# Four moves in the order of work of a two-layer decoder trunk: the first weight block, the second triangular inverse, the last products of v, and the last norm

## The chip, the cores and the metric

The kernel runs on one core of one Trainium2 chip, as one program that is launched once. A core has a matrix engine (TensorE, "PE" in the profile, with its weight loads shown apart as "PEld"), a vector engine (DVE), a scalar engine (ACT), a general engine (POOL), a queue engine (SP) that here only issues DMAs, and 16 DMA engines. Each engine runs its own list of instructions strictly in order; an instruction that waits holds back all that stand behind it on the same engine. The metric is the device time of one execution in microseconds (us), median over executions; lower is better.

## The reference

The input is 512 tokens of 1024 numbers. Layer 0 is an RG-LRU block and layer 1 an RWKV-7 block; each is followed by a gated convolution MLP, and a last RMS norm ends it. Cut to what matters here:

```python
h = rmsnorm(x);  u = h @ w_in + b_in                    # RG-LRU: the first products of the kernel
...                                                     # conv, gates, scan, w_out, residual, MLP 0
r, k, v = (h + xx * mix[i]) @ w_rkv[i]  for i in 0,1,2  # RWKV-7
for t in tokens:                                        # state S of 64 x 64 for each of 16 heads
    S = S * w[t] + (S @ a[t]) b[t]^T + v[t] k[t]^T
    y[t] = S @ r[t]
y = groupnorm(y) * ln_w + ln_b + bonus * v              # the norm: 64 numbers of a head and token
x = x + (y * g) @ w_out                                 # then MLP 1 and the last norm
```

The recurrence is computed in chunks of 64 tokens. In a chunk the tokens depend on each other through a triangular matrix of 64 x 64 for each head, whose inverse is needed before the chunk can be done.

## The kernel before, in words

**Products.** Every large product is taken in three passes (`mm3`, lines 46 to 53): the weight and the activation are each split in a high part (a cast on ACT, line 90) and a low part (a subtraction on DVE, line 91), and PE adds high x high (L51), high x low (L52) and low x high (L53). Weights come by DMA in blocks of 512 KB ("raw", L148), are split into "wh" and "wl", and are used by `project_gen` (L172), which walks over blocks of 256 rows (`c`), four output banks (`o`) and the two halves of a block (`k`). `next_weights` (L165) asks for the loads of the next three blocks and the split of the next two each time a block is taken.

**The order of the work.** The program is written as generators that are interleaved by hand: `push(task, lane)` puts one into one of three lists, and `background(n, lane)` takes n pieces from the first task in that list. In the chunk steps the amounts are in `self.fills`: three lanes, and for each the pieces taken at three places in a step. What is written in this way is the priority only. A planner then lays out the list of each engine: it plays the program through with its own costs, gives a free engine the earliest written of the instructions that it takes to be ready, and hands out the buffers (`b4`, 21 of 4 KB a partition; PSUM, eight banks). So a list can differ from the written order where the planner believed that a transfer or another engine would be done earlier or later. `keep_in_program_order` ties an instruction behind the one written before it on its engine.

**Start.** `load_x` (L308) issues the loads of x (`xin`, four pieces, the first in two halves) and of the first weights in turn. The input is transposed on PE into "xT" (L344), block by block of 128 of the 1024 features, and then split on ACT (L346) and DVE (L347) into "xs". `warm` (L332) puts transposes of the identity on PE that nothing uses. `lru` (L359) does block 0, splits weight block 0 in two halves, calls `warm(WARM2)`, does block 1, and pushes blocks 2 to 7 as a task for the first products.

**Inverse.** `solve(H)` (L997) makes the inverses for one half of the heads: eight groups of small products ("aab", L1020) with copies on ACT (L1025, L1028), a transpose on DVE (L1033), a chain of 31 pairs of DVE operations (L1041, L1043), two more DVE transposes (L1046, L1048), and two rounds of small products ("m1p" L1065, "ltp" L1077). The tiles of the first inverse are named D and A, those of the second DA.

**Products of v.** `tokens(g)` (through `project_tokens`, L977) computes v for all tokens and a quarter of the features: 96 products (L989 to L991), given out in 16 pieces of six. Groups 0 and 1 are done before the chunk steps, groups 2 and 3 are pushed to lane 1 as cover for the steps.

**Chunk steps.** There are 16 chunks of work (8 for each half H of the heads; `NC` is 8) and two groups of heads, the second one chunk behind the first, so 17 steps (`step`, L1190). The chain in a step is: "pe" on PE (L1206), a copy on ACT (L1209), "pu" on PE (L1222), a copy on ACT (L1229, tile "tu"), "pd" on PE (L1238), two operations on DVE (L1247, L1248 or L1250, tile "sv"), and the next "pe". Between them PE does "s", "tr" and "py". After every second step a `tail` (L1262) is begun: the group norm of 128 tokens, in three parts: mean, square and variance, with a power on POOL (L1278); three DVE operations (L1281 to L1283); transposes on PE ("pz", L1288) with ACT copies (L1291). `trail` moves each open tail one part on, in the next steps.

**End of the block.** `first_half` (L1362), pushed in lane 1 after step 9, multiplies the first half of y by the gate ("pgt" on PE, "yg" on DVE at L1356, split into "BK") and runs its 96 output products, in 20 pieces; the second half follows after the last step, from line 1421 to line 1441.

## Time and profile before

| what | value |
|---|---|
| median of 3 runs | 1327.06 us (1325.48 to 1329.35) |
| the profiled execution, its own time | 1328.46 us |
| its span, first to last instruction | 1326.7 us |
| so around the span | 1.76 us |
| mean granted PE clock | 0.992 |
| PE busy | 1295.2 us, 98% |
| DVE busy | 860.3 us, 65% |
| ACT busy | 614.0 us, 46% |
| POOL busy | 67.9 us, 5% |
| DMA | 120.27 MB, mean 91 GB/s |

Times inside the profile count from the start of the span. In the rows with several columns each engine has its busy time and, in brackets, its number of instructions in the stretch; "PEclk" is the granted clock as a share of full speed. "[3.35 <-DMA xin]" behind an instruction says that its engine had stood idle for 3.35 us and what ended that. PE is shown as busy at half clock too, so a lower clock has to be read in its own column.

### The profile page before, as it was taken

To read this page: it belongs to the slowest core of one execution; us is meant where nothing else is said; L and a number is where in the kernel's file an instruction comes from. 1 tells how busy PE (TensorE), PEld (TensorE's weight loads), DVE (VectorE), ACT (ScalarE), POOL (GpSimd) and SP (SyncE) were. 2 spreads that over 40 slices of the span, in tenths; PEclk is the share of its full clock that TensorE was granted. 3 is DMA by queue.
4 is the path that set the end of the run, shared out by engine and by line. 5 is a ranking of instruction groups with operands and counts; after the bars stand their busy time and mean duration, and the time that the engine had idled before them with its cause. 6 is when DMAs were issued, how large, how long until landed. Compare 5 with 4: busy or idle time off the path is not lost.

```text
span 1326.7 us, 20245 instructions
## 1 busy us (share of the span) xinstructions
PE 1295.2 (98%) x8339; PEld 1055.3 (80%) x8339; DVE 860.3 (65%) x1332; ACT 614.0 (46%) x968; POOL 67.9 (5%) x110
## 2 busy tenths in 40 slices
PE   8999999999999999999999988799999999999998
PEld 7877888888888888876678877678888888888886
DVE  5998656455436655497989787877565555365523
ACT  6797444333224423368843668555533332244311
POOL 4000000000000000020010011120000000000000
PEclk8999999999999999999999999899999999999999
DMA  5423333323333433213212112133323223333311
GB/s 183 126 64 96 96 111 96 95 64 96 95 96 95 127 115 120 88 32 116 86 48 72 58 38 80 42 89 91 99 89 109 67 95 95 96 96 127 112 64 64
DMA packets 72124, 120.27 MB, mean 91 GB/s; under 512 B 9498, under 2 KB 21476, under 8 KB 71904
## 3 DMA queue, kind: packets, MB, share of 16 engines
q1 hardware_dynamic: 70672, 117.20, 28.7%
q8 instruction: 65, 1.06, 0.3%
q10 hardware_dynamic: 576, 1.05, 0.2%
q0 software_dynamic: 784, 0.74, 0.2%
q14 instruction: 27, 0.22, 0.1%
HBM read 114.44 MB, written 4.52 MB: 90 GB/s over the span
## 4 chain that ended last, share of the span: by engine, by line
PE 88%; DVE 6%; ACT 3%; issue 1%; DMA 1%; POOL 0%; SPq 0%; POOLq 0%; DVEq 0%; ACTq 0%
PE acc L51 22%; PE acc L53 22%; PE acc L52 22%; PE acc L616 3%; PE acc L615 3%; PE acc L617 3%; PE s L1160 1%; PE acc L989 1%; PE acc L990 1%; PE acc L991 1%; PE pe L1206 1%; DVE W L1167 1%; DMA xin<-in_x_dram 1%; DVE X L1043 1%; DVE sv L1248 1%
## 5 line engine op out<-in xcount | busy, mean ns | idle before, releaser
L51 PE MATMUL acc<-xs,wh 128*128 128x512 f32 x896 | 352.0, 393 | 0.0
L53 PE MATMUL acc<-xs,wl 128*128 128x512 f32 x896 | 348.9, 390 | 0.7 <-DVE wl L91 0.7
L52 PE MATMUL acc<-xs,wh 128*128 128x512 f32 x896 | 349.6, 390 | 0.0
L91 DVE TENSOR_TENSOR wl<-raw,wh 128x1024 fp32r<-128x1024 f32 (+1 forms) x201 | 242.9, 1216 | 163.4 <-PE acc L52 95.0
L90 ACT CAST wh<-raw 128x1024 fp32r<-128x1024 f32 (+1 forms) x201 | 207.9, 1045 | 257.7 <-DVE wl L91 169.6
L53 PEld LDWEIGHTS acc<-xs,wl 128*128 128x128 f32 x896 | 168.5, 188 | 36.8 <-DVE wl L91 1.2
L51 PEld LDWEIGHTS acc<-xs,wh 128*128 128x128 f32 x896 | 168.8, 188 | 35.0 <-ACT wh L90 0.2
L52 PEld LDWEIGHTS acc<-xs,wh 128*128 128x128 f32 x896 | 168.7, 188 | 34.5 <-DVE wl L91 0.2
L576 DVE SCALAR_TENSOR_TENSOR cv<-gpad,pv,cv 128x512 f32<-128x512 f32 x96 | 71.9, 749 | 22.2 <-ACT cv L574 21.1
L90 ACT CAST hid<-un 128x512 fp32r<-128x512 f32 x48 | 29.8, 620 | 108.7 <-DVE un L583 108.7
L616 PE MATMUL acc<-wh,hid 128*128 128x512 f32 (+1 forms) x200 | 76.8, 384 | 0.0
L615 PE MATMUL acc<-wh,hid 128*128 128x512 f32 (+1 forms) x200 | 76.5, 382 | 0.0
L617 PE MATMUL acc<-wl,hid 128*128 128x512 f32 (+1 forms) x200 | 75.9, 380 | 0.0
L52 PE MATMUL acc<-hid,wh 128*128 128x512 f32 x192 | 75.7, 394 | 0.0
L53 PE MATMUL acc<-hid,wl 128*128 128x512 f32 x192 | 75.6, 394 | 0.0
L51 PE MATMUL acc<-hid,wh 128*128 128x512 f32 x192 | 75.5, 393 | 0.0
L582 DVE TENSOR_TENSOR un<-acc,rb 128x512 f32<-128x512 f32 x48 | 33.1, 689 | 44.3 <-PE acc L53 44.3
L91 DVE TENSOR_TENSOR hid<-un,hid 128x512 fp32r<-128x512 f32 x48 | 33.2, 691 | 31.5 <-ACT hid L90 31.5
L574 ACT ACTIVATE cv<-gpad,pv 128x512 f32<-128x512 f32 x48 | 39.2, 817 | 20.3 <-DVE gpad L571 20.1
L578 ACT ACTIVATE ge<-cv 128x512 f32<-128x512 f32 x48 | 30.1, 627 | 35.6 <-DVE cv L576 35.6
L620 DVE TENSOR_TENSOR xtok<-xtok,acc 128x512 f32<-128x512 f32 (+1 forms) x25 | 16.7, 666 | 44.9 <-PE acc L617 44.9
L615 PEld LDWEIGHTS acc<-wh,hid 128*128 128x128 f32 x200 | 37.5, 188 | 8.0
(425 smaller groups left out, 2176.1 us busy)
## 6 DMA issues: line engine op xcount, KB each, us to landing
raw<-in_ffn_w_up_dram SPq DMA_DIRECT2D x96, 512.0 KB, 3.9
raw<-in_ffn_w_down_dram SPq DMA_DIRECT2D x48, 512.0 KB, 3.7
raw<-in_rwkv_w_rkv_dram SPq DMA_DIRECT2D x24, 512.0 KB, 3.8
raw<-in_lru_w_in_dram SPq DMA_DIRECT2D x16, 512.0 KB, 3.9
raw<-in_lru_w_out_dram SPq DMA_DIRECT2D x8, 512.0 KB, 3.8
raw<-in_rwkv_w_out_dram SPq DMA_DIRECT2D x8, 512.0 KB, 3.4
xd<-x SPq DMA_DIRECT2D x8, 256.0 KB, 2.0
AR<-xd SPq DMA_DIRECT2D x1, 2048.0 KB, 9.1
```

The source lines that it names most:

```text
L51: nc.tensor.matmul(ps, wh, xh, start=start, stop=False)
L52: nc.tensor.matmul(ps, wh, xl, start=False, stop=False)
L53: nc.tensor.matmul(ps, wl, xh, start=False, stop=stop)
L90: (self.nc.vector.tensor_copy if dve else self.nc.scalar.copy)(hi, src)
L91: self.nc.vector.tensor_tensor(lo, src, hi.bitcast(F32), ALU.subtract)
L574: nc.scalar.activation(cv, gp[:, 0:T], AF.Identity, bias=self.vec(f"ffn_conv_b{l}", fb), scale=cw(0))
L576: nc.vector.scalar_tensor_tensor(cv, gp[:, j : j + T], cw(j), cv, ALU.mult, ALU.add)
L578: nc.scalar.activation(ges[o], cv, AF.Gelu_apprx_tanh)
L582: nc.vector.tensor_tensor(un, ps, rbs[0], ALU.mult)
L615: nc.tensor.matmul(ps, hh[:, s], wh[:, k, m], start=kk == 0, stop=False)
L616: nc.tensor.matmul(ps, hl[:, s], wh[:, k, m], start=False, stop=False)
L617: nc.tensor.matmul(ps, hh[:, s], wl[:, k, m], start=False, stop=kk == 7)
```

## The change

- The pad `WARM2` goes from 4 to 20 transposes. Block 1 of x is no longer done ahead of the first products: with the new argument `early`, the first products of weight block 0 run for `k` = 0 over all four banks, and block 1 is written after the second of these banks. The call of `next_weights`, which also splits weight block 1, is thereby written ahead of block 1.
- The second inverse is pushed after the seventh piece of the first group of v, where it was pushed at the start of the second group: ten calls of `background` earlier, each with 0.8 pieces for lane 2.
- Step 7 no longer asks for all of v first, only that one task is left in lane 1; the last group of v may run on in step 7, and what is left of it is taken at the first place of step 8. The fills of steps 0 to 6 go from 3.8 to 3.4 pieces in lane 1 and from 5.1 to 4.5 in lane 2. In steps 10 and 11 lane 1 gets 2.8 pieces for 2.1 before; from step 12 on 2.1 as before.
- The last tail is split by groups of heads: one for the first two blocks after step 15, one for the other two after step 16, each with half the elements. Gate products of blocks 4 and 5 are multiplied ahead of the third part of the second of them.

```diff
-WARM2 = 4
+WARM2 = 20
...
-    def project_gen(self, xs, evac, nob=4, kb=8, kc=2, join=2):
+    def project_gen(self, xs, evac, nob=4, kb=8, kc=2, join=2, early=None):
...
             ws = [self.next_weights() for _ in cs]
+            if early and cs[0] == 0:
+                (wh, wl), = ws
+                for o in range(nob):
+                    self.mm3(pss[o], (wh[:, 0, o * P : (o + 1) * P], wl[:, 0, o * P : (o + 1) * P]), xs[0], True, False)
+                    if o == 1:
+                        early()
             for o in range(nob):
                 for c, (wh, wl) in zip(cs, ws):
-                    for k in range(kc):
+                    for k in range(1 if early and c == 0 else 0, kc):
...
             warm(WARM2)
-            block(1)
...
-                self.project(xs, lambda o, ps: take(g * 4 + o, ps), after=None if g else first, rate=1.2, join=2 if g else 1)
+                self.project(xs, lambda o, ps: take(g * 4 + o, ps), after=None if g else first, rate=1.2, join=2 if g else 1,
+                             early=None if g else lambda: block(1))
...
-        def tail(H, c2):
-            y = ytok[H, c2].rearrange("p b (h i) -> p (b h) i", h=2)
+        def tail(H, c2, b0=0, nb=4):
+            hs = slice(2 * b0, 2 * (b0 + nb))
+            y = ytok[H, c2][:, b0 : b0 + nb].rearrange("p b (h i) -> p (b h) i", h=2)
...
         for g in range(2):
-            if g:
-                self.push(self.solve(1, AR, BK, LTs), 2)
             for i, _ in enumerate(tokens(g)):
+                if g == 0 and i == 6:
+                    self.push(self.solve(1, AR, BK, LTs), 2)
...
-        self.fills = ((1.2, 1.1, 0.2), (1.0, 0.9, 1.9), (1.3, 1.8, 2.0))
+        self.fills = ((1.2, 1.1, 0.2), (0.9, 0.8, 1.7), (1.1, 1.6, 1.8))
...
         for n in range(N + 1):
-            while n == NC - 1 and self.tasks[1]:
+            while n == NC - 1 and len(self.tasks[1]) > 1:
                 self.background(1, 1)
             if n == NC:
-                self.drain()
-                self.fills = ((2.9, 0.5, 2.3), (0.8, 0, 1.3), (0, 0, 0))
+                for lane in (0, 2):
+                    while self.tasks[lane]:
+                        self.background(1, lane)
+                self.fills = ((0, 0, 0), (32, 0, 0), (0, 0, 0))
             if n == NC + 1:
                 load_lnw(1)
+                self.drain()
+            if n > NC:
+                self.fills = ((0, 0, 0), (1.2, 0, 1.6) if n < NC + 4 else (0.8, 0, 1.3), (0, 0, 0))
             step(n, trail)
             m = n - 1
-            if m > 0 and m % 2:
+            if n >= N - 1:
+                tails.append(tail(1, NC // 2 - 1, 2 * (n - N + 1), 2))
+                next(tails[-1])
+            elif m > 0 and m % 2:
                 tails.append(tail(m // NC, m % NC // 2))
                 next(tails[-1])
...
         trail()
         gp = [gate_mm(b) for b in range(4, 8)]
-        self.background(3, 1)
+        self.background(2.5, 1)
+        for i in range(2):
+            gate_mul(4 + i, gp[i])
         trail()
-        self.background(1, 1)
-        gate_mul(4, gp[0])
         self.drain()
-        for i in range(1, 4):
+        for i in range(2, 4):
             gate_mul(4 + i, gp[i])
```

More of the change, by code (lines that the diff above doesn't have):

```diff
@@ L1260, in step @@
             fill(2)
-        def tail(H, c2):
-            y = ytok[H, c2].rearrange("p b (h i) -> p (b h) i", h=2)
-            wide = lambda ap: ap.unsqueeze(2).to_broadcast([P, 8, C])
-            sm = lambda name: self.xsp.tile([P, 8, C], F32, tag="sq", name=name, bufs=3)
-            mu, var = (pool.tile([P, 8], F32, tag=k, name=k, bufs=2) for k in ("mu", "var"))
+        def tail(H, c2, b0=0, nb=4):
+            hs = slice(2 * b0, 2 * (b0 + nb))
+            y = ytok[H, c2][:, b0 : b0 + nb].rearrange("p b (h i) -> p (b h) i", h=2)
+            wide = lambda ap: ap.unsqueeze(2).to_broadcast([P, 2 * nb, C])
+            sm = lambda name: self.xsp.tile([P, 8, C], F32, tag="sq", name=name, bufs=3)[:, 0 : 2 * nb]
+            mu, var = (pool.tile([P, 8], F32, tag=k, name=k, bufs=2)[:, 0 : 2 * nb] for k in ("mu", "var"))
             self.need(("bonus", H))
@@ L1272, in tail @@
             nc.scalar.activation(sq, y, AF.Square)
-            vv = V[:, c2, H * 512 : H * 512 + 512].rearrange("p (b i) -> p b i", i=C)
+            vv = V[:, c2, H * 512 + b0 * P : H * 512 + (b0 + nb) * P].rearrange("p (b i) -> p b i", i=C)
             bv = sm("bv")
-            nc.gpsimd.tensor_tensor(bv, vv, wide(bons[H][:, c2, :]), ALU.mult)
+            nc.gpsimd.tensor_tensor(bv, vv, wide(bons[H][:, c2, hs]), ALU.mult)
             nc.vector.tensor_reduce(var, sq, AX.X, ALU.add)
             nc.vector.tensor_scalar(var, var, 1.0 / C, GN_EPS, ALU.mult, ALU.add)
-            nc.gpsimd.tensor_tensor(mu, var, self.mhalf.to_broadcast([P, 8]), ALU.pow)
+            nc.gpsimd.tensor_tensor(mu, var, self.mhalf.to_broadcast([P, 2 * nb]), ALU.pow)
             yield 1
             tc.keep_in_program_order(nc.vector.tensor_tensor(y, y, wide(mu), ALU.mult))
-            nc.vector.tensor_tensor(y, y, lnws[H], ALU.mult)
+            nc.vector.tensor_tensor(y, y, lnws[H][:, hs], ALU.mult)
             nc.vector.tensor_tensor(y, y, bv, ALU.add)
@@ L1285, in tail @@
             pz = self.bank("pz")
-            for i in range(4):
-                put = tc.keep_in_program_order if i == 0 else lambda ins: ins
+            for i in range(b0, b0 + nb):
+                put = tc.keep_in_program_order if i == b0 else lambda ins: ins
                 put(nc.tensor.transpose(pz[:, i * P : (i + 1) * P], ytok[H, c2][:, i, :], self.ident))
-            for i in range(4):
+            for i in range(b0, b0 + nb):
                 b = H * 4 + i
```

## The prediction, made before the changed kernel was run

> **What bounds the kernel now.** I read the page's busy shares first, then PE's own list of waits over the whole span.
>
> ```profile
> PE 1295.2 (98%) x8339; PEld 1055.3 (80%) x8339; DVE 860.3 (65%) x1332; ACT 614.0 (46%) x968; POOL 67.9 (5%) x110
> ```
> ```profile
> PE pe L1206 <- DVE sv L1248: 6.7, 7, 2.9
> PE pd L1238 <- ACT tu L1229: 4.9, 6, 1.5
> PE xT L344 <- DMA xin<-in_x_dram: 3.3, 1, 3.3
> PE pz L1288 <- DVE ytok L1283: 2.9, 1, 2.9
> ...
> PE m1p L1065 <- DVE XN L1048: 1.5, 1, 1.5
> ...
> PE acc L53 <- DVE wl L91: 0.7, 1, 0.7
> ```
>
> PE is the bound, and no part of the change takes a product away. So it can only pay through PE's idle time, 1326.7 - 1295.2 = 31.5 us, and through time at half clock. The long waits are those of the chunk steps, and 3.3 us at the start. Third I cut the chunk steps at the start of each "pe" and looked at the two stretches ahead of them. The columns are the stretch, its length, then busy time of PE, PEld, DVE, ACT and POOL, the granted clock, and the DMA share and rate.
>
> ```profile
> 727.20:735.30 8.10, 8.09 (x183) 7.25 (x184) 1.80 (x3) 6.10 (x14) 3.37 (x4) 1.00 0.22 67
> ...
> 740.06:747.07 7.01, 7.01 (x117) 6.33 (x116) 6.71 (x17) 4.08 (x10) 0.00 (x0) 1.00 0.07 13
> 747.07:757.34 10.27, 8.60 (x160) 6.19 (x159) 9.67 (x24) 5.25 (x12) 0.00 (x0) 1.00 0.21 73
> 757.34:767.15 9.81, 9.50 (x160) 8.53 (x161) 9.26 (x22) 4.49 (x12) 1.04 (x1) 0.83 0.21 63
> 767.15:779.06 11.91, 8.96 (x171) 8.25 (x171) 11.35 (x29) 7.04 (x14) 2.65 (x2) 1.00 0.31 89
> 779.06:788.83 9.77, 9.42 (x165) 8.79 (x165) 6.39 (x13) 5.90 (x15) 1.99 (x2) 0.83 0.01 2
> 788.83:799.39 10.56, 8.57 (x169) 7.99 (x170) 10.27 (x19) 8.91 (x17) 1.63 (x1) 1.00 0.17 53
> 799.39:809.41 10.02, 8.48 (x276) 7.57 (x276) 9.55 (x15) 7.01 (x18) 0.31 (x1) 1.00 0.02 4
> 809.41:818.45 9.04, 8.95 (x265) 6.48 (x264) 6.43 (x13) 7.24 (x18) 2.94 (x3) 1.00 0.02 4
> ...
> 832.72:842.53 9.81, 8.33 (x142) 6.59 (x141) 5.05 (x11) 5.42 (x15) 1.04 (x1) 0.77 0.23 67
> 842.53:851.25 8.72, 6.38 (x141) 4.91 (x141) 8.53 (x18) 6.03 (x14) 1.63 (x1) 1.00 0.17 59
> ```
>
> The rows from 740.06 are steps 0 to 7, then 10 and 11. PE idles (length less busy) 1.7, 0.3, 3.0, 0.4, 2.0 and 1.5 us in steps 1 to 6, together 8.8; 0.1 in step 7; 1.5 and 2.3 in steps 10 and 11. After the long idle of steps 1 and 3 the clock of the next step is 0.83, a third of it at half clock, so 0.17 of 9.8 us, 1.7 us each, is lost beside. DVE is the engine that is nearly full in steps 1, 2 and 3 (30.3 of 32.0 us), and it stands idle for 6.3 us of the 8.1 just ahead of them.
>
> **The first weight block.** Here are the rows of the start, from the timeline, and the clock by single microseconds (columns: stretch, length, PE busy, clock, DMA).
>
> ```profile
> 1.43 3.14 PE L332 MATMUL warm<-ident 128*128 128x128 f32 x14 [1.43 <-POOL ident masks.py:199]
> 5.15 0.60 PE L332 MATMUL lnps<-ident 128*128 128x128 f32 x4
> 6.65 1.14 ACT L90 CAST wh<-raw 128x512 fp32r<-128x512 f32 x2 [0.61 <-DMA raw<-in_lru_w_in_dram]
> 7.30 1.29 DVE L91 TENSOR_TENSOR wl<-raw,wh 128x512 fp32r<-128x512 f32 x2 [0.48 <-ACT wh L90]
> 9.10 1.11 PE L344 MATMUL xT<-ident,xin 128*128 128x128 f32 x4 [3.35 <-DMA xin<-in_x_dram]
> 10.25 0.69 ACT L346 ACTIVATE xs<-xT,ln 128x512 fp32r<-128x512 f32 x1 [1.98 <-PE xT L344]
> 11.96 1.04 ACT L90 CAST wh<-raw 128x1024 fp32r<-128x1024 f32 x1 [1.02 <-DMA raw<-in_lru_w_in_dram]
> 12.16 0.63 PE L51 MATMUL acc<-xs,wh 128*128 128x512 f32 x1
> 12.59 0.63 PE L52 MATMUL acc<-xs,wh 128*128 128x512 f32 x1
> ...
> 18.55 0.39 PE L52 MATMUL acc<-xs,wh 128*128 128x512 f32 x1
> 18.78 0.40 PE L53 MATMUL acc<-xs,wl 128*128 128x512 f32 x1
> ```
> ```profile
> 8.00:9.00 1.00, 0.00 (x0) 0.50 1.10 381
> 14.00:15.00 1.00, 1.00 (x5) 0.71 1.07 356
> ```
>
> A product takes 0.43 us at half clock (12.16 to 12.59) and 0.23 at full (18.55 to 18.78). The hole of 3.35 us halves the clock until 14 to 15 us. A pad of 20 at 0.15 each (0.60 for 4) fills 5.15 to 8.2 at most. The first weights are split by then (7.30 plus half of 1.29 is 7.95), so the twelve products with k = 0 run at full clock from about 8: six until 9.4, block 1's transposes (x lands at 9.10), six more until 11.2. Before, one product had started by 10.25 and the block ended at 19.0. With xs of block 1 split at once (9.6 + 0.69 on ACT + 0.75 on DVE) the twelve others would be through by 14 and with the transposes at 15.5: 3.5 us won.
>
> But ACT's list changes too: weight block 1's cast is now written ahead of block 1's xs. The planner takes transfers to be done early (it put the transposes of 9.10 where PE then stood 3.35 us). With as much optimism it takes weight block 1, which came at 11.96, to be there at 8.6, before xs (9.6 at the earliest). Then ACT, in order, stands until 11.96 with xs behind it; xs is ready at 11.96 + 1.04 + 0.69 = 13.7, PE waits for it some 2.5 us, and the twelve others end at 16.5, or at 18.9 if that hole halves the clock again. I hold this three times as likely as the good order. What passes on is what DVE's start moves, for DVE is full behind it:
>
> ```profile
> DVE wl L91 <- ACT wh L90: 3.0, 2, 2.8
> ```
>
> This is all but 0.2 us of its waits from 24 to 83 us, and the first later wait of PE is the 0.7 us for wl (above). So I take -1.3 us for this part, with -3.5 and +0.5 as ends (the lower end from no gap, the upper one for the pad and a second halving).
>
> The pad hangs on one rule. The Trainium skill, "TensorE: Matmul & The Clock Gate", Part 4: PE-mode transpose, says that transposes do not count as PE work for the clock. This trace disagrees: 14 transposes alone take 3.14 us, 0.22 each, and those from 5.15 on 0.15. By the rule the twelve first products would cost 12 x 0.20 = 2.4 us more and the sum below would be -2.6.
>
> **The second inverse.** Its rows in the timeline, and DVE's chain by groups from 735 to 774 us:
>
> ```profile
> 717.25 0.46 PE L1020 MATMUL aab<-AR,BK 64*64 64x64 f32 x16
> 717.86 0.28 PE L990 MATMUL acc<-wh,mix 128*128 128x256 f32 x1
> 717.98 0.28 PE L991 MATMUL acc<-wl,mix 128*128 128x256 f32 x1
> ...
> 735.37 1.97 DVE L1033 STREAM_TRANSPOSE DA<-DA 128x1024 f32<-128x1024 f32 x1 [3.94 <-ACT DA L1028]
> ```
> ```profile
> L1041 DVE TENSOR_TENSOR DA<-DA,X 128x31 f32<-128x31 f32 (+15 forms) x31 | 10.6, 341 | 0.9
> L1043 DVE TENSOR_TENSOR X<-X,DA 128x31 f32<-128x31 f32 (+15 forms) x31 | 10.6, 341 | 1.0
> ```
>
> Nothing is added. The eight groups of aab (8 x 0.46 = 3.7 us of PE, full there either way) and twelve ACT copies come ten calls earlier, each with about six products of 0.12 us and an aab: some 8 us. The chain's start, 735.37, moves to about 727, into DVE's idle stretch. 6.3 of the 21.2 us of the chain leave steps 0 to 3, where the waits for sv arise. The POOL fills of X move with it and POOL is 5% busy; no DMA moves. The most it can give is all idle of steps 1 to 6 and the two halvings, 8.8 + 3.4 = 12.2 us. It can also cost: moved DVE work may land ahead of an sv elsewhere, and the longest such wait is 2.9 us. I take half of the idle of steps 1 to 3 (5.0) and half of a halving: -3.3, nearer the low end, since the three 2 us transposes of this chain still stand somewhere among the steps.
>
> **The last group of v.** 0.4 pieces less in each of steps 0 to 6 is 2.8 pieces of 6 x 0.12 = 2.0 us of PE work that goes to steps 7 and 8. Step 7 has 0.1 us idle, so there it is on the path. What it takes off ahead counts only where PE does not wait. So between 0 and +2.0; the two weight splits that go with the group (an ACT cast and a DVE subtraction each, L90 and L91) leave fuller steps. I take +0.6.
>
> **The last steps.** 1.4 more pieces in steps 10 and 11, each six products of 0.23, move 1.9 us of PE work from behind step 16 into 3.8 us of idle. A gate piece brings DVE two operations in step 11, where DVE is full (8.53 of 8.72), so I take -1.0, ends -1.9 and +1.7. The +1.7 is the cover lost at the end:
>
> ```profile
> 894.55 0.60 PE L1288 MATMUL pz<-ident,ytok 128*128 128x128 f32 x4
> ...
> 897.45 1.29 DVE L91 TENSOR_TENSOR BK<-yg,BK 128x512 fp32r<-128x512 f32 x2
> ```
>
> After the last pz PE has 18 products of `first_half` left (4.1 us, until 899.0), and the two first blocks of the second half are split by 898.7. So the cover was just used up; 1.9 us less of it opens a gap unless the chain from the last "py" gets shorter. The split does that: the first two blocks begin a step earlier, at the end of step 15 and not of step 16, one step or about 5.5 us; the others work on half the elements. The extra instructions of the second tail, seven on DVE, one on ACT, two on POOL, lie beside full PE work.
>
> **The sum.** -1.3 - 3.3 + 0.6 - 1.0 = -5.0 us. On the profiled execution's own 1328.46 us (span 1326.7 and 1.76 around it) this gives 1323.5. It lies 1.4 above the median of the runs shown, so on the median, 1327.06, the forecast is **1322.0 us**.
>
> **The rivals.**
>
> *Everything is had* (1313). The good order on ACT (-3.5), three quarters of the 12.2 us of steps 1 to 6 (-9.2) and -1.0: -13.7, so 1313.4. For it speaks that DVE's idle stretch is as long as the waits it should take away; against it that the waits for "tu" (4.9 us) end on ACT, which the change does not relieve.
>
> *Nothing is had* (1326). The start loses its gain behind ACT's early cast (0), the idle of the steps only changes its place (-1.0), the rest cancels out: -1. For it speaks that the planner fills lists by its own belief, so a freed engine need not free the instruction that PE waits for.
>
> *The pad does not hold the clock*, the rule above: -2.6, so 1324.5.
>
> *The steps starve* (slower, 1332). One mechanism: thinner fills in steps 1 to 6. A step with less cover than its chain idles, and an idle like the 1.7 us of step 1 or the 3.0 us of step 3 halves the clock in the next step, 1.7 us each. It decides once three more steps idle so: 3 x 1.7 and the 2.0 us of fill that then count in step 7 without being saved before make +7.1; the start's -1.3 and the end's -1.0 leave +4.8, so 1331.9. For it: two of six steps did so with the thicker fill. Against it: steps 2, 4 and 6 hold with 1.5 us of idle or less.
>
> **How the numbers follow.** Chances: the forecast with its own range of 1317.5 to 1324.5, 0.47; everything 0.15; nothing 0.20; the pad's rule 0.05; starving 0.13. A median of this kernel tells a change from none at about 0.3%, 4 us, so faster is below 1323.1 and slower above 1331.0. Faster: 0.4 of the forecast's 0.47 and all of "everything", 0.55. Slower: most of "starving", 0.10. Between them 0.35. The ends of all terms together are -17.6 and +7.1 (the inverse with its longest wait, +2.9, the others as above); the range that leaves 0.2 out cuts half of "everything" and most of "starving": 1314 to 1329.
>
> **What would show it.** The start: the clock stays 1.00 from 4 to 11 us, products begin near 8; right in the bad order if ACT's cast of the second weight block comes before the second xs and PE shows a hole before 13.7, wrong if xs comes first. The inverse: DVE busy in nearly all of the stretch before step 0, the chain L1041 ending some 8 us earlier against step 0, and less than 5 us of waits for sv in steps 1 to 6; wrong if these are as long as before. The last group: products of v inside step 7 or 8, step 7 longer by up to 2 us. The end: no PE idle between step 16 and the first products of the second half, and less in steps 10 and 11. The whole is wrong if the steps 0 to 7 take as long as before or longer, or if the start gives nothing.

## The result, and the profile after

The changed kernel takes 1334.29 us (median of 4 runs, 1333.06 to 1335.55), the kernel before beside it 1327.42. The ratio is 1.0051, 95% interval 1.0036 to 1.0066: slower by 6.9 us, where 1322.0 was forecast, and outside the range of 1314 to 1329. The profiled execution took 1335.55 us, its span is 1333.8.

The page's first rows and PE's own waits over the whole span (us in total, times, longest):

```profile
PE 1299.3 (97%) x8355; PEld 1057.1 (79%) x8355; DVE 862.6 (65%) x1339; ACT 614.2 (46%) x969; POOL 69.6 (5%) x112
```
```profile
PE pz L1296 <- DVE ytok L1291: 6.7, 2, 3.7
PE pe L1213 <- DVE sv L1255: 5.4, 6, 2.0
PE pd L1245 <- ACT tu L1236: 4.1, 6, 1.5
PE pe L1213 <- DVE sv L1257: 2.5, 2, 2.0
PE acc L51 <- ACT xs L353: 2.4, 1, 2.4
PE m1p L1072 <- DVE XN L1055: 1.5, 2, 0.8
```

The span grew by 7.1 us: PE is busy 4.1 us longer and idles 3.0 longer. The products are the same; the count is 16 higher by the transposes of the longer pad, which take some 1.8 us of the 4.1 (2.35 us for 20, before 0.60 for 4), and the rest is half clock. The wait for "xin" of 3.3 us is gone; a wait for "xs" of 2.4 and a second wait for "ytok" of 3.7 are new. The waits for "sv" (5.4 and 2.5; before 6.7 and 1.7) are hardly shorter.

To place the 7.1 us I compared the start of the same products in both profiles. The later the changed kernel is, by place: +1.3 us behind the start, and the same until step 0 begins (741.36 against 740.06); +1.4 at step 8; +3.1 at step 16 (884.31 against 881.20); +7.0 at the first product of the second half (906.20 against 899.18). The 1.7 us between steps 8 and 16 are not a loss by themselves: 12 more products of the first half (2.8 us) are done there, and they are missing as cover behind step 16.

**Start.** PE, then ACT of the changed kernel, from the timeline:

```profile
10.73 0.40 PE L53 MATMUL acc<-xs,wl 128*128 128x512 f32 x1
13.53 0.50 PE L51 MATMUL acc<-xs,wh 128*128 128x512 f32 x1 [2.41 <-ACT xs L353]
...
16.30 0.63 PE L52 MATMUL acc<-xs,wh 128*128 128x512 f32 x1
```
```profile
11.85 1.04 ACT L90 CAST wh<-raw 128x1024 fp32r<-128x1024 f32 x1 [3.88 <-DMA raw<-in_lru_w_in_dram]
12.80 0.68 ACT L353 ACTIVATE xs<-xT,ln 128x512 fp32r<-128x512 f32 x1
```

The first products begin at 7.67 and run at full clock, as forecast. Then ACT stands 3.88 us at the cast of the second weight block with "xs" behind it, PE stands 2.41 us, and the product of 16.30 takes 0.43 us to the next, half clock.

**Steps.** The stretch of 727.20 before step 0 in the changed kernel, and the rows of its steps 0 to 3 and 0 to 7 (length, busy time of PE, PEld, DVE, ACT, POOL, clock, DMA); then the sum over steps 0 to 7 of the kernel before:

```profile
727.20:735.30 8.10, 7.35 (x139) 6.75 (x138) 7.72 (x14) 5.29 (x7) 1.90 (x2) 1.00 0.14 48
...
741.36:747.66 6.30, 6.30 (x111) 5.61 (x110) 6.03 (x14) 3.15 (x8) 0.00 (x0) 1.00 0.01 4
747.66:759.70 12.04, 9.58 (x166) 7.05 (x165) 11.28 (x29) 5.25 (x12) 0.00 (x0) 1.00 0.18 50
759.70:769.33 9.63, 7.32 (x154) 6.43 (x155) 9.07 (x21) 5.04 (x13) 0.82 (x1) 1.00 0.39 118
769.33:779.34 10.01, 8.81 (x157) 7.96 (x157) 5.97 (x13) 6.39 (x14) 4.77 (x5) 0.83 0.08 23
...
741.36:819.87 78.51, 69.88 (x1478) 59.20 (x1477) 63.99 (x129) 48.62 (x112) 10.85 (x10) 0.98 0.14 40
```
```profile
740.06:818.45 78.39, 69.49 (x1477) 60.14 (x1476) 69.63 (x146) 49.92 (x115) 10.57 (x10) 0.96 0.14 40
```

```profile
729.34 2.02 DVE L1040 STREAM_TRANSPOSE DA<-DA 128x1024 f32<-128x1024 f32 x1
```
```profile
PE pe L1213 <- DVE sv L1255: 3.2, 2, 2.0
PE pe L1213 <- DVE sv L1257: 2.5, 2, 2.0
```

(The last two fences are the changed kernel's: the start of the second inverse's chain in DVE's timeline, and PE's waits for "sv" between 747 and 803 us.) DVE is now busy in the stretch ahead of step 0 (7.72 us, before 1.80), and has 5.6 us less to do in the steps. Against the start of step 0, its chain begins 7.3 us earlier and its last operation (765.1; before 773.7) comes 9.9 us earlier. The steps still take 78.5 us. Steps 1 and 2 idle 2.5 and 2.3 us, and step 3 runs a third at half clock.

**End.** PE behind step 16 in the changed kernel, DVE and POOL beside it, and the two stretches of the wait and of what follows:

```profile
889.59 0.40 PE L53 MATMUL acc<-BK,wl 128*128 128x512 f32 x1
893.70 0.66 PE L1296 MATMUL pz<-ident,ytok 128*128 128x128 f32 x2 [3.72 <-DVE ytok L1291]
894.01 0.78 PE L51 MATMUL pgt<-tgs,g2h 128*128 128x512 f32 x1
894.59 0.63 PE L52 MATMUL pgt<-tgs,g2h 128*128 128x512 f32 x1
895.01 0.63 PE L53 MATMUL pgt<-tgs,g2l 128*128 128x512 f32 x1
...
899.93 0.40 PE L53 MATMUL pgt<-tgs,g2l 128*128 128x512 f32 x1
900.16 0.40 PE L1359 MATMUL pgt<-tgs,g2s 96*128 96x512 f32 x1
900.40 0.40 PE L51 MATMUL acc<-BK,wh 128*128 128x512 f32 x1
```
```profile
891.67 0.41 DVE L1290 TENSOR_TENSOR ytok<-ytok,lnw 128x256 f32<-128x256 f32 x1
892.01 1.21 DVE L91 TENSOR_TENSOR wl<-raw,wh 128x1024 fp32r<-128x1024 f32 x1
893.15 0.41 DVE L1291 TENSOR_TENSOR ytok<-ytok,bv 128x256 f32<-128x256 f32 x1
```
```profile
888.38:891.80 3.42, 1.61 (x10) 1.07 (x8) 2.69 (x8) 2.56 (x6) 1.59 (x2) 1.00 0.14 29
891.80:899.00 7.20, 5.30 (x14) 4.26 (x15) 5.24 (x11) 2.06 (x5) 1.01 (x1) 0.57 0.17 61
```

The first half tail's two "pz" stand on PE ahead of the sixteen gate products, which need nothing from that tail. PE waits 3.72 us, and the gate products then run at half clock, 13 of the 16 (0.57 in that stretch). 1.1 us of the wait is a weight block's subtraction that DVE does at 892.01, between the last two operations of the tail. In the kernel before, the single tail's "pz" stood behind the gate products.

### The profile page after: what moved, and what is told of

It reads as the page before. It is cut to its first block, busy times and chain, and to the rows that moved or that the text cites. A ratio compares the mean times of both kernels' runs of the same rounds, so it can differ in the third digit from the quotient of the medians.

```text
span 1333.8 us, 20292 instructions
## 1 busy us (share of the span) xinstructions
PE 1299.3 (97%) x8355; PEld 1057.1 (79%) x8355; DVE 862.6 (65%) x1339; ACT 614.2 (46%) x969; POOL 69.6 (5%) x112
## 4 chain that ended last, share of the span: by engine, by line
PE 86%; DVE 7%; ACT 4%; issue 2%; DMA 1%; POOL 0%; SPq 0%; POOLq 0%; DVEq 0%; ACTq 0%
PE acc L51 22%; PE acc L53 22%; PE acc L52 22%; PE acc L623 3%; PE acc L622 3%; PE acc L624 3%; DVE X L1050 1%; PE s L1167 1%; DVE DA L1048 1%; DVE wl L91 1%; DMA raw<-in_lru_w_in_dram 1%; PE acc L996 1%; PE pe L1213 1%; DVE W L1174 1%; DVE sv L1255 0%
## 5 line engine op out<-in xcount | busy, mean ns | idle before, releaser
L53 PE MATMUL acc<-hid,wl 128*128 128x512 f32 x192 | 75.6, 394 | 0.0
L581 ACT ACTIVATE cv<-gpad,pv 128x512 f32<-128x512 f32 x48 | 39.2, 817 | 20.3 <-DVE gpad L578 20.1
L578 DVE TENSOR_TENSOR gpad<-acc,rb 128x512 f32<-128x512 f32 x48 | 32.9, 686 | 19.6 <-PE acc L53 19.5
```

What stands on the lines that cost most here:

```text
L53: nc.tensor.matmul(ps, wl, xh, start=False, stop=stop)
L578: nc.vector.tensor_tensor(gp[:, 2:], ps, rbs[0], ALU.mult)
L581: nc.scalar.activation(cv, gp[:, 0:T], AF.Identity, bias=self.vec(f"ffn_conv_b{l}", fb), scale=cw(0))
```

## The experiments

All ratios are to the kernel before, timed beside it on the same chip; 0.001 is 1.3 us. The right column is the ratio times 1328 us, less 1328.

| kernel | ratio | 95% interval | us |
|---|---|---|---|
| start_only | 1.0003 | 0.9990 to 1.0017 | +0.4 |
| pad_only | 0.9979 | 0.9966 to 0.9992 | -2.8 |
| start_mended | 0.9980 | 0.9967 to 0.9993 | -2.7 |
| inverse_only | 0.9974 | 0.9962 to 0.9986 | -3.5 |
| inverse_fills | 0.9981 | 0.9969 to 0.9994 | -2.5 |
| inverse_last_v | 0.9960 | 0.9945 to 0.9974 | -5.3 |
| inverse_covers | 0.9984 | 0.9973 to 0.9994 | -2.1 |
| covers_only | 1.0007 | 0.9993 to 1.0020 | +0.9 |
| end_only | 1.0005 | 0.9992 to 1.0018 | +0.7 |
| after_old_end | 0.9995 | 0.9983 to 1.0007 | -0.7 |
| after_old_end_fill | 1.0002 | 0.9992 to 1.0011 | +0.3 |
| after_old_late_fill | 1.0031 | 1.0020 to 1.0042 | +4.1 |
| after_end_mended | 0.9993 | 0.9983 to 1.0004 | -0.9 |
| after_one_piece | 0.9999 | 0.9988 to 1.0009 | -0.1 |
| after_thick_fills | 0.9967 | 0.9954 to 0.9979 | -4.4 |
| start_mended_inverse | 0.9966 | 0.9954 to 0.9977 | -4.5 |
| sm_inv_end | 0.9954 | 0.9940 to 0.9969 | -6.1 |
| after_three_mends | 0.9942 | 0.9923 to 0.9962 | -7.7 |

### The start

**start_only**: the kernel before with the change's pad, `early` and block(1) inside the first products, and nothing else.

> The kernel before with the first part of the change alone: the pad of 20, block 1 of x inside the first products, and with it the split of weight block 1 written ahead of block 1. Theory (order on ACT): PE stands idle from about 11.1 to 13.5 us because ACT waits for weight block 1 (11.9 us) with the second xs behind it, and the products from 30 us on start 1.0 to 1.5 us later than before; time +1.3 us, between 0 and +2.5 as the clock falls. Rival (the whole loss of 7 us at the end of the block comes from the start, by another phase of the steps): +4 to +7.

**pad_only**: one number.

```diff
-WARM2 = 4
+WARM2 = 20
```

> The kernel before with WARM2 20 for 4 and nothing else: products still wait for block 1 of x at 9.1 us. Theory (transposes hold the clock): clock 1.00 from 4 to 11 us and on, the first products 0.23 us apart, about 2 us won by 20 us, time -1 to -2 us. Rival (transposes do not count for the clock): clock 0.5 from about 8 to 14 us as before, products 0.43 us apart, time within 0.5 us of before.

**start_mended**: the start of the change, and the split of weight block 1 (cast on ACT, subtraction on DVE) written behind block 1's xs.

```diff
-            ws = [self.next_weights() for _ in cs]
+            ws = [self.next_weights(not (early and c == 0)) for c in cs]
...
                     if o == 1:
                         early()
+                        self.weights_split(self.n_used + 1)
```

> As start_only, but weight block 1 is split behind block 1 of x, so that ACT has the second xs first. Theory (order on ACT): no hole of PE over 0.5 us after the pad, the clock stays full, products with the second xs begin near 11 us, and from 30 us on all starts 2.5 to 3.5 us earlier than before; time -2.5 to -3.5 us. Rival (DVE, full from 24 to 82 us, sets the pace of PE there): the lead is lost again by 83 us and the time is within 1 us of before.

Here is ACT of start_mended from the timeline, and then the stretch from 11 to 20 us, first of start_mended and then of the changed kernel:

```profile
10.84 0.69 ACT L355 ACTIVATE xs<-xT,ln 128x512 fp32r<-128x512 f32 x1 [1.44 <-PE xT L353]
12.01 1.05 ACT L90 CAST wh<-raw 128x1024 fp32r<-128x1024 f32 x1 [0.48 <-DMA raw<-in_lru_w_in_dram]
```
```profile
11.00:20.00 9.00, 9.00 (x52) 7.31 (x51) 5.99 (x8) 8.08 (x22) 4.22 (x9) 1.00 0.83 272
```
```profile
11.00:20.00 9.00, 5.87 (x24) 4.54 (x24) 3.39 (x4) 4.26 (x7) 4.11 (x8) 0.81 0.79 260
```

With xs first PE has no hole at all, at the same landing of the weight block (12.01 against 11.85). The order on ACT is what takes the start's gain; it is worth about 3 us (from +0.4 to -2.7, each known to some 1.7 us). PE's wait for "wl" at 80 us stayed (0.7), but the lead was not lost there (2.9 us at the first inverse's first DVE transpose, 667.8 against 670.7): DVE moved along, so it was not the floor I had taken it for.

pad_only gains as much as the whole mended start, so the pad is what pays, and the products block by block add nothing to it that can be seen. The execution that was profiled is the slowest of its twelve (1330.86 us), so its profile shows what the pad does at the start, and the gain rests on the timing alone. In its profile PE's transposes fill 5.72 to 8.18, the hole is 0.60 us, and the clock stays full:

```profile
5.72 2.46 PE L332 MATMUL lnps<-ident 128*128 128x128 f32 x20
8.77 0.66 PE L344 MATMUL xT<-ident,xin 128*128 128x128 f32 x4 [0.60 <-DMA xin<-in_x_dram]
```
```profile
5.00:15.00 10.00, 9.33 (x59) 7.87 (x58) 4.76 (x7) 5.46 (x9) 6.16 (x13) 1.00 1.02 329
```

So transposes hold the clock, against the rule of the Trainium skill ("TensorE: Matmul & The Clock Gate", Part 4: PE-mode transpose) that was one of my rivals: that rival is out.

### The inverse, the fills and the last group of v

**inverse_only**: the second `solve` pushed at the sixth call of group 0, as in the change; nothing else.

> The kernel before with the second inverse pushed in the first group of v and nothing else (fills 3.8 and 5.1 as before). Theory (the wait only changes its place): the chain on DVE starts 6 to 8 us earlier, PE's waits for sv in steps 1 to 6 still sum to 5 us or more, time within 1.5 us of before. Rival (the thinner fills of the change ate the gain of the earlier inverse): waits for sv under 3 us and time -3 us or better.

Measured -3.5 us, where -3.3 was forecast. PE's waits for "sv" in steps 1 to 6 are 4.0 us in its profile (before 5.6), between the two readings. Over steps 0 to 7 PE idles 7.6 us (before 8.9) and the clock is 1.00 (before 0.96). The three kernels below then add what the change does to the cover. "Fills" is

```diff
-        self.fills = ((1.2, 1.1, 0.2), (1.0, 0.9, 1.9), (1.3, 1.8, 2.0))
+        self.fills = ((1.2, 1.1, 0.2), (0.9, 0.8, 1.7), (1.1, 1.6, 1.8))
```

and "last group" is

```diff
-            while n == NC - 1 and self.tasks[1]:
+            while n == NC - 1 and len(self.tasks[1]) > 1:
...
-                self.drain()
-                self.fills = ((2.9, 0.5, 2.3), (0.8, 0, 1.3), (0, 0, 0))
+                for lane in (0, 2):
+                    while self.tasks[lane]:
+                        self.background(1, lane)
+                self.fills = ((0, 0, 0), (32, 0, 0), (0, 0, 0))
```

**covers_only**: fills and last group, without the earlier inverse.

> Of the kernel before, with the thinner fills of lane 1 and lane 2 and with the last group of v going on into steps 7 and 8, and nothing else of the change. Theory (the thinner cover is what ate the gain of the earlier inverse): it costs something of itself too, since steps 1 to 6 then idle more or step 7 has 2 us more of products: ratio 1.001 to 1.003, and the gaps ahead of pe, pd in steps 1 to 6 sum to more than the 8.8 us of before. Rival 1 (cover is only in the way of DVE where the inverse has moved; without the earlier inverse the step is bound by DVE and thinner cover costs nothing): 0.999 to 1.0005, with products moved to step 7 filling it. Rival 2 (the part is a gain of itself, and it is its meeting with the earlier inverse that is bad): below 0.998.

**inverse_fills**: the earlier inverse and the fills.

> The kernel before with the earlier second inverse, which alone gave 0.9974, and the thinner fills; the last group of v is still finished before step 7, as in the kernel before. Theory A (thin fills are the loss): the gain goes, 0.999 to 1.001. Theory B (the products of v inside steps 7 and 8 are the loss): the gain stays, 0.9970 to 0.9980, for what the thin fills leave over is then done ahead of step 7 with nothing between. The kernel with both and the new start, but the old end, had 1.0002, and the start alone 1.0003, so the two parts together have nothing left of the inverse's 3.5 us.

**inverse_last_v**: the earlier inverse and the last group.

> The kernel before with the earlier second inverse and with the last group of v going on into steps 7 and 8, with the old, thicker fills. Theory (the last group's products in steps 7 and 8, with the two weight splits, are what costs): 2 to 3 us of the inverse's 3.5 gone, ratio 0.999 to 1.000. Rival (only both together cost, for with the thicker fills little is left for step 7): 0.997 to 0.9985.

**inverse_covers**: the earlier inverse, the fills and the last group.

> The kernel before with the earlier second inverse, the thinner fills and the last group of v in steps 7 and 8; start and end as before. If these two parts take the inverse's gain as they did beside the new start: 0.9995 to 1.0005 (-0.1 us by difference of the runs so far). If it was the new start that took it (its 1.3 us lag shifts the planner's lists): 0.997 to 0.998.

My theory that the last group costs is refuted: with it and the old fills the gain is 5.3 us, not less than 3.5. The theory that thin cover costs without the earlier inverse is not borne out, though not excluded: +0.9, with an interval that holds zero. What costs is the thinner fills beside the earlier inverse: 0.9960 against 0.9984, 3.2 us, known to some 2.4. Without the last group the step (0.9974 to 0.9981) is 0.9 us and within the uncertainty.

**after_thick_fills**: the changed kernel with the gate products written ahead of pz (below) and the old fills; the kernel it is to be compared with is after_end_mended.

> The changed kernel with the gate products written ahead of the first half's pz, and with the fills of steps 0 to 6 as thick as before. The start is that of the change. With the gate products ahead alone it was 0.9993. Theory (the thinner fills cost 2.5 to 3.2 us beside the earlier inverse: inverse with last group 0.9960, the same with thin fills 0.9984): 0.9965 to 0.9975. Rival (the changed start's lag shifts the lists so that this gain does not show): 0.9985 to 0.9995.

0.9967 against 0.9993: 3.5 us again, now inside the whole change. Its stretches for steps 2, 3, and 0 to 7:

```profile
757.77:766.85 9.08, 7.97 (x161) 7.12 (x161) 8.51 (x18) 5.08 (x11) 0.82 (x1) 1.00 0.31 96
766.85:775.87 9.02, 8.43 (x166) 7.65 (x166) 6.31 (x13) 6.42 (x17) 4.77 (x5) 1.00 0.18 59
...
738.75:814.36 75.61, 67.64 (x1477) 57.80 (x1476) 65.92 (x132) 48.85 (x113) 10.85 (x10) 1.00 0.14 42
```

Step 2 idles 1.1 us instead of 2.3 (step 1, on the other hand, 3.1 instead of 2.5), and step 3 keeps the full clock (0.83 in the changed kernel): 9.02 us instead of 10.01. Steps 0 to 7 take 75.6 instead of 78.5. PE's idle time over them differs by only 0.7 us (7.97 and 8.63); the other 2.2 us are PE busy longer, 1.7 of them by the clock of step 3 (0.17 of 10.0). But this half clock does not come in every execution. after_one_piece (below) has the thin fills and the same wait in step 2, and its steps 2 and 3 are

```profile
758.33:767.97 9.64, 7.32 (x155) 6.44 (x155) 9.08 (x21) 5.04 (x13) 0.82 (x1) 1.00 0.39 126
767.97:776.45 8.48, 7.28 (x157) 6.57 (x157) 5.98 (x13) 6.38 (x14) 4.77 (x5) 1.00 0.07 21
```

There the clock stays 1.00, step 3 takes 8.48 us, and steps 0 to 7 take 77.3. Over all seven profiles with the earlier inverse, the thin fills and the last group, steps 0 to 7 take 76.6 to 78.7 us: two have the half clock in step 3, four in step 1, and after_one_piece has none. In the three with the old fills (inverse_last_v, after_thick_fills, after_three_mends) they take 75.6 to 75.8. So in these steps the thin fills cost 0.8 to 3.1 us, 1.7 where neither side has half clock.

### The end

**after_old_end**: the changed kernel with the old single tail and the old order behind the last step.

> The changed kernel with the end of before: one last tail after step 16 and the old order behind it (3 pieces, trail, 1 piece, four gate multiplications); the fills of steps 10 and 11 stay at 2.8. Theory (pz ahead of cover): no pz waits ahead of the gate products, so the idle of 3.7 us is gone, but the cover at the end is 1.9 us shorter: idle of 1 to 2 us there, time 2 to 4 us below the changed kernel. Rival (cover): the same idle of about 4 us at the end.

**after_old_end_fill**: and the old fills in steps 9 to 11.

> As after_old_end, and the fills of steps 10 and 11 also as before (2.1 pieces). Theory: no idle at the end, as before; steps 10 and 11 together 1.6 us shorter than in the changed kernel; what is left is the start (+1.3 us) and the steps (0), so the time is +1 to +2 us against before. Rival (the earlier inverse and the thinner fills cost by themselves): +3 us or more.

**after_old_late_fill**: the changed kernel with the old fills in steps 9 to 11, the new end kept.

```diff
-                self.fills = ((0, 0, 0), (1.2, 0, 1.6) if n < NC + 4 else (0.8, 0, 1.3), (0, 0, 0))
+                self.fills = ((0, 0, 0), (0.8, 0, 1.3), (0, 0, 0))
```

> The changed kernel with the fills of steps 10 and 11 as before (2.1 pieces) and the new end kept. Theory (pz ahead of cover): the wait before pz stays at 3 to 4 us, for the order on PE is the same, and the time is within 1.5 us of the changed kernel. Rival (cover): with 1.9 us more of output products left, the wait falls by 1.9 us or more and the time by 3 us.

**after_end_mended**: the changed kernel with two lines exchanged.

```diff
-        trail()
         gp = [gate_mm(b) for b in range(4, 8)]
+        trail()
         self.background(2.5, 1)
```

> The changed kernel with one move: the gate products of blocks 4 to 7 are written ahead of the trail that puts the first half tail's pz on PE. Theory (pz ahead of cover): PE's idle of 3.7 us before pz near 890 us is filled by the 16 gate products, the clock is not halved there, time 3.5 to 5 us below the changed kernel, so about +2 us against before. Rival (the cover itself is too short, for 1.9 us of it was taken in steps 10 and 11): an idle of 2 us or more stays before the first products of the second half, and the time falls by less than 2 us.

Taking the old end, or exchanging those two lines, brings the kernel from 1.0051 back to 0.9995 and 0.9993: the new end costs 7 to 8 us, and it does so by this order, given how little cover stands ahead of pz. The fuller steps 9 to 11 do not make the wait: without them the kernel still has a wait of 3.72 us and 1.0031. What they are worth themselves stays unclear: taking them out gave -2.7 us with the new end and +0.9 with the old. (At the same wait of 3.72 us, 8 of the 16 gate products ran at half clock in the profile of after_old_late_fill, and 13 in the changed kernel's.) In after_old_end the old chain has the shorter cover, and PE idles 0.49 us behind step 16, where 1 to 2 were expected. Of after_end_mended, PE behind step 16:

```profile
888.49 0.39 PE L53 MATMUL acc<-BK,wl 128*128 128x512 f32 x1
888.72 0.39 PE L51 MATMUL pgt<-tgs,g2h 128*128 128x512 f32 x1
...
892.21 0.39 PE L1359 MATMUL pgt<-tgs,g2s 96*128 96x512 f32 x1
892.60 0.41 PE L1296 MATMUL pz<-ident,ytok 128*128 128x128 f32 x2
892.77 0.48 PE L51 MATMUL acc<-BK,wh 128*128 128x512 f32 x1
```

The gate products fill the time in which DVE ends the tail, and pz waits for nothing.

**end_only**: the kernel before with the split norm, the changed order and the fuller fills, to see the cost by itself.

> The kernel before with the last norm split in two halves, the new order behind the last step and the thicker fills of lane 1 in steps 9 to 11; start, inverse, fills and last group of v as before. Theory (the first half's pz is put on PE ahead of the sixteen gate products and PE stands until its DVE rows are done): 1.004 to 1.006, with one gap of 3 to 4 us ahead of pz behind step 16 and a clock below 1.00 in the 7 us after it. Rival (the gap only comes about because in the whole change the steps end later on DVE): below 1.001, no gap over 1 us there.

This missed: +0.7 us, within the uncertainty, not +6. The order on PE is the same, but 16 products of the first half instead of four stand between the last "py" and pz (887.85 to 891.42 in its timeline), the wait is 0.93 us and the clock stays full. So the order alone does not cost 7 us; it makes PE wait for whatever the cover ahead does not fill. How many pieces are ahead hangs on the fractions that `background` carries: in the changed kernel 0.8 left over from step 9, 2 x 2.8 and 5 x 2.1 add up to 16.9 by the end of step 16, so 16 pieces are given out. In end_only 0.9 is left over, the sum is 17.0, and 17 pieces are given out.

**after_one_piece**: the changed kernel with 0.2 of a piece more in step 16.

```diff
-(0.8, 0, 1.3)
+(0.8, 0, 1.3 if n < N else 1.5)
```

> The changed kernel with one number changed: in step 16 the last fill of lane 1 is 1.5 instead of 1.3. The fractions carried from step to step then pass a whole number one step place earlier, and 12 more products of the first half (12 x 0.23 = 2.8 us) stand on PE ahead of the pz of the first half tail; the gate products still stand behind it. Theory (the wait's size is set by the cover ahead of it, and the clock halves only from some 3 us of wait on): the gap shrinks from 3.72 to about 0.9 us, the clock stays 1.00 in the 7 us after it, 6 us less than the changed kernel, ratio 0.999 to 1.001. Rival (the order itself costs, since the gate products that stand behind pz are late for yg and the second half's products whatever the gap): 1.003 to 1.005, with a new gap ahead of the first products of the second half.

```profile
889.89 0.40 PE L53 MATMUL acc<-BK,wl 128*128 128x512 f32 x1
891.21 0.41 PE L1296 MATMUL pz<-ident,ytok 128*128 128x128 f32 x2 [0.92 <-DVE ytok L1291]
```
```profile
891.00:899.00 8.00, 7.79 (x36) 6.41 (x37) 6.11 (x14) 3.32 (x8) 1.01 (x1) 1.00 0.24 69
```

(Two rows of its PE timeline, and the stretch behind.) The wait falls from 3.72 to 0.92 us, the clock stays 1.00, and the kernel is 6.9 us faster than the change (0.9999 against 1.0051, a difference known to some 2.4). One piece is six products; on PE's list 12 more stand ahead of pz, 16 where there were 4, so the list moved by more than the piece. With 2.8 us of wait gone, the other part is the clock: the sixteen gate products take 6.4 us in the changed kernel (894.01 to 900.40) and 3.8 here, 2.6 us less; together 5.4, and the rest is within the uncertainty. From the start of step 16 to the first product of the second half the profiles have 21.9 us in the changed kernel, 16.4 here and 15.4 in after_end_mended. The rival "the order itself costs", which put this kernel at 1.003 to 1.005, is refuted; the 1.0 us by which after_end_mended is shorter there does not show in the times (0.9993 and 0.9999). That "the clock halves only from some 3 us of wait on" is not borne out either: the last section has a wait of 1.78 us that lost it.

### The parts together

**start_mended_inverse**: the mended start and the earlier inverse in the kernel before.

> The kernel before with two parts: the start with the split of weight block 1 written behind the second xs (0.9980 alone, -2.6 us) and the earlier second inverse (0.9974 alone, -3.5 us). If parts so far from each other add up: -6.1 us, ratio 0.9954, 0.994 to 0.9965, faster than both kernels. If the start's lead is only lent and is lost in front of the chunk steps because something there comes at its own time: 0.9970 to 0.9980, the inverse's gain alone.

**sm_inv_end**: with the split norm and its mended order too.

> The kernel before with the mended start, the earlier second inverse, and the split last norm with the gate products written ahead of its first pz; fills up to step 8 and the last group of v as before. Start and inverse together gave 0.9966. If the mended end is worth nothing (it was 0.3 us apart from the old end in the changed kernel): 0.996 to 0.997. If the fuller steps 10 and 11 and the split pay once the gap is gone, as forecast (-1.0 us): 0.9955 to 0.996.

**after_three_mends**: the changed kernel with the split of weight block 1 behind xs, the old fills in steps 0 to 6, and the gate products ahead of pz.

> The changed kernel with three mends: gate products ahead of pz, thick fills, and the split of weight block 1 written behind the second xs. Sum of the parts: start -2.6, inverse with last group of v -5.3, end about 0: -7.9 us, ratio 0.994, 0.993 to 0.9955, the fastest so far. If the start's lead of 2.6 us does not add up with the rest: 0.996 to 0.9975.

start_mended_inverse lies at the edge of what both readings gave (0.9966; the sum 0.9954 is the end of its interval), so it decides nothing but that the two together are faster than the kernel before. after_three_mends has 0.9942, as its parts add up to (0.994); PE is busy 1293.1 us in its profile, 98% of the span. It is 12 us faster than the changed kernel (1321.98 against 1334.29 us, though not timed side by side) and 7.7 faster than the one before, known to some 2.6: with three faults of order and amount mended, the change is a gain. With sm_inv_end (0.9954) it overlaps, so that the last group of v is worth anything beside the rest is likely, not shown.

## Why the prediction was wrong, point by point

**The bound** held: PE at 97 to 98%, and the gains and losses that were placed are idle time or half clock of PE.

**The start** (forecast -1.3, ends -3.5 and +0.5; timed alone +0.4). The mechanism was right down to the rows: cast before xs, ACT standing until 11.85, PE's hole until 13.53 (forecast 13.7). The step that missed is the price: I gave the bad order a chance of three to one and still took a gain of 1.3 us for it (which lies at the edge of the interval of +0.4). The hole halves the clock again in this profile, and even my end for that case, 18.9, was early: the block ends at 20.3 (20.09 and 0.23), since PE waits 0.72 us more at 14.86, for the low part of xs, which stands behind the weight block's subtraction on DVE too (12.92), and runs transposes of the next blocks at half clock too. The other half of the miss is the kernel before: its profile has a hole of 3.35 us, and in six other profiles with the old start PE waited only 0.9 to 2.7 us for "xin", with the clock from 4 to 24 us between 0.83 and 1.00.

**The inverse** (-3.3; timed alone -3.5, beside the last group -5.3). Right in size and place: DVE busy in the stretch before step 0, the chain's first transpose at 729.34 instead of 735.37, 7.3 us earlier against step 0, where 8 were worked out, and its end 9.9 earlier. The sign "less than 5 us of waits for sv in steps 1 to 6" held with the inverse alone (4.0) and failed in the whole change: 5.7 us from 747 to 803, as long as before (5.6).

**The last group of v and the fills** (+0.6, ends 0 and +2.0). I priced the two as one move of 2.0 us of products into step 7. They are two things: with the old fills the last group is no cost (-5.3 with it, -3.5 without, a difference within the uncertainty), while the thinner fills cost 3.2 to 3.5 us beside it. The working "what it takes off ahead counts only where PE does not wait" left out that cover taken off a waiting step lengthens the wait and can halve the clock of the next one. That is my own rival "the steps starve", with the right mechanism (steps 2 and 3 above) at about half its price (3.2 to 3.5 us for 7.1), and with the half clock of 1.7 us once or, in after_one_piece, not at all, instead of three times.

**The end** (-1.0, ends -1.9 and +1.7; measured +7 to +8). This is the step that failed and that decides the sign. I worked out whether the chain from the last "py" would fit behind 1.9 us less cover, and argued that the split makes it shorter. The chain is shorter, but the step looked only at the chain's length: PE's list was not read. The diff moves no `trail()`, yet with the split that same `trail()` puts out the first half's pz, which before came with the next one, behind the gate products. So 16 products (3.7 us) of cover that needed nothing went behind the wait. And no price for a halved clock at the end was in the ends of the term; +1.7 should have been about +6 (3.7 us of wait, 2.6 of half clock). The fear behind the +1.7, that 1.9 us less cover opens a gap with the old chain, was nearly empty: after_old_end idles 0.49 us there.

**The sum.** Measured in parts: +0.4 for the start, -3.5 for the inverse, +1.4 for fills and last group beside it (inverse_covers less inverse_only), so -1.7 without the end's order, where after_end_mended has -0.9; the difference is within the uncertainty. The order at the end adds +7.7 (1.0051 less 0.9993), which is read from the changed kernel itself: +6.0, against 6.9 measured. None of my rivals had this. The slower one came near with 1332, but that is luck: its place was the steps.

**What stays open**: how the 3.2 us of the thinner fills divide in other executions between waits and clock (the profiles of inverse_last_v and inverse_covers, the pair that was timed, differ by only 0.8 us in steps 0 to 7, and both have a stretch at half clock), and how much of the last group's 1.8 us is real.

## What to carry to other kernels

When a task is split into two, follow each line that advances tasks and see on the in-order engine's list what now comes out of it earlier, and which work without needs stands behind. Price a wait of some 2 us or more with the half clock that may follow it, as a step and not a slope: here 0.2 of a piece more put 12 products ahead of a wait and was worth 6.9 us. And give out cover in counts that do not hang on a carried fraction, or lay the independent work ahead of the wait, where it serves as cover whatever the count.

## What the runs showed of the hardware that I had not expected

The same start gives a different hole in each execution. In eight profiles with the changed start the second weight block's cast began between 10.75 and 12.24 us, since its transfer landed then, and the following lead or lag against the profile of before (at the first inverse's first DVE transpose, 670.7 us there) was between -1.4 and +2.7 us. The old start scatters as well: six profiles with it (inverse_only, inverse_fills, inverse_last_v, inverse_covers, covers_only, end_only) lead the profile of before by 0.3 to 2.4 us at the same place. So the +1.3 us found above behind the start is no more than one execution's difference from another.

A longer hole does not always halve the clock. Here are PE's waits in the same place, and the stretches behind, of after_one_piece and then of start_only:

```profile
13.72 0.50 PE L51 MATMUL acc<-xs,wh 128*128 128x512 f32 x1 [2.08 <-ACT xs L353]
```
```profile
14.57:20.00 5.43, 4.94 (x29) 4.19 (x30) 2.79 (x5) 3.99 (x7) 1.16 (x3) 1.00 0.62 201
```
```profile
13.60 0.50 PE L51 MATMUL acc<-xs,wh 128*128 128x512 f32 x1 [1.78 <-ACT xs L353]
```
```profile
14.57:20.00 5.43, 5.06 (x21) 4.09 (x22) 1.81 (x3) 2.55 (x5) 1.25 (x3) 0.69 0.59 183
```

2.08 us of wait kept the full clock and 1.78 lost it; and the same 2.3 us in step 2 were followed by half clock in the changed kernel and by full clock in after_one_piece. This fits what the Trainium skill says ("TensorE: Matmul & The Clock Gate", Part 1), that the clock is set by a window of 3.4 us that runs freely and does not begin with the kernel's work; these runs show the scatter, not the window itself. For a forecast it means that a lead or lag after a hole, read from one profile, is known to some 2 us only.
